# A two-layer hybrid diffusion step on one core: the second layer's modulation on VectorE, first loads as long rows, equal slots, and operands at chosen places of 256 bytes

## The chip, the cores and the metric

The kernel runs on one core of one Trainium2 chip. The time is device microseconds of one execution. The kernel before was run three times: 1936.15, 1937.8 and 1947.53 us, so its median is 1937.8 us. The profiled execution is a fourth run; times inside the trace (its span) are a little shorter than the device's own time for the same execution.

## The reference, cut to what matters

Two layers work on 384 tokens (128 context tokens, which are modulated by `c_ctx`, and 256 latent tokens, modulated by `c`) of 1024 channels. Each layer is

```python
shift1, scale1, gate1, shift2, scale2, gate2 = split(adaLN of c)
h = rms_norm(x) * (1 + scale1) + shift1
x = x + gate1 * mix(h)        # SSD, attention and mLSTM side by side, gated, one output projection
h = rms_norm(x) * (1 + scale2) + shift2
a, b = split(h @ w_ffn_in)    # 2 x 2816 wide
x = x + gate2 * ((silu(a) * b) @ w_ffn_out)
```

The six modulation vectors of a layer ("adaLN") are `silu(c) @ w_ada + b_ada`, with a matrix of 1024 x 6144 for each layer and two vectors (context and latent). All of it is float32.

## The kernel before, in words

A `Recorder` notes every operation first. `order()` then plays them through with its own list of costs and waiting times (`cost`, `LAT`, a model of TensorE's clock, one of the port that VectorE and GpSimd share, one of the DMA ring), takes on each engine the operation with the smallest key (its place in the program plus the `urgency` around it: FEED for loading and splitting weights, EVAC for emptying PSUM, DENSE for large products), and so writes down an order for each engine, which the chip then keeps. All instructions are issued from one line of `emit`, so the profile shows one line for all of them and is read by the names of tiles.

All weights stand in one array `in_ws` of pieces of 128 x 1024 float32 (512 KB), in the order in which `stream()` lists them. `piece()` loads a piece into one of four `raw` tiles; ACT rounds it to `wh` (the high part), and VectorE, or GpSimd for every n-th piece of the kinds in `POOL_SPLIT`, writes the rest to `wl`. A dense product of 128 output channels (`dense_t`) is 24 matmuls: eight chunks of 128 input channels, each `wh` by the activations' high part, `wh` by their low part and `wl` by their high part. The activations lie in large tiles by pairs (`HH`/`HL` for the mixers' input, `A`/`C` for the FFN's, `PH`/`PL` for a branch). There are three PSUM tiles `d` for dense products, four `m` and one `l` for small ones.

A layer goes through: early gates and the input projections with the three mixers between them (their steps taken by turns as the string `MIX` says: s is one group of two SSD heads, a attention, m mLSTM, q and i inputs), the three branch projections (`br`), the output projection (`outproj`), the FFN's first half (`fa` and `fb`, 22 times two dense products) and its second half (`fo`). After each dense product of the FFN's first half VectorE takes it out of PSUM times the norm (`sc<-d,nacc`); the product of the halves is again split into a high part (ACT) and a low part (VectorE), in the tiles `D`, `E`, `F`, `F2`, `B`, `HH`, `HL`.

The adaLN has three forms. Four units of layer 0 (`ada`: shift1 and scale1) are computed at the very start, because the first product needs them. The rest of layer 0 (`ada_step`, 16 steps) is spread over the branch and output projections, and all of layer 1 (`ada_step`, 24 steps) over the FFN of layer 0. A step takes two pieces and is four matmuls of the two modulation vectors (`silc`, as stationary operand, 32 columns) by 512 columns of weights in float32, side by side in four column groups of the array; after eight steps the result is transposed back and `b_ada` is added.

At the start, `setup` loads the small inputs and `x` (tile `PH`), the sums of squares of `x` run on ACT and VectorE (`ssq`, `norm_end`), the first four `ada` units come in through the four `raw` tiles, and `modulate` makes `HH`/`HL` chunk by chunk.

Of the kernel before, what the change touches and what calls it, by code (L numbers as in the profile page):

```python
# [21 lines left out]
LAYERS = 2  # L22
FFN = 2816
FT = FFN // P
EPS = 1e-6
# [5 lines left out]

EARLY_GATES = (0, 1, 2, 4, 5, 5, 6, 6, 6, 10, 11, 13, 13, 23, 32, 32, 32, 33, 33, 37, 37, 37, 37, 38)

# [30 lines left out]
def stream():  # L64

    s = [(("ada", 0, u), 4) for u in (0, 2, 1, 3)]
    steps = lambda l, *gs: [(("ada", l, g, k), 2) for g in gs for k in range(KT)]
    for l in range(LAYERS):
        early = iter(gates())
        s += [(("gate", l) + next(early), 1) for _ in range(FIRST_GATES if l else 0)]  # L70
        s += [(("dtmg", l), 1)]
        base = [(("in", l, OFF[n] + j * P), 1) for n in ("sx", "sb", "sc") for j in range(2 if n != "sx" else 8)]
        base += [(("inn", l, OFF["aq"] + j * 512), 4) for j in range(3)]
        base += [(("in", l, OFF[n] + j * P), 1) for n in ("mq", "mk") for j in range(8)]
        base += [(("inn", l, OFF["mv"] + j * 512), 4) for j in range(2)]
# [12 lines left out]
    return s  # L88
# [134 lines left out]
class Recorder:  # L223
# [122 lines left out]
    def cost(eng, meth, args, kw):  # L346
# [7 lines left out]
        if eng == "vector":  # L354
            if meth == "reciprocal":
                return 0.07 + n * 0.0062
            if meth == "tensor_reduce":
                n = _free(args[1])
            if meth == "tensor_scalar" and not args[1].buf.psum:
                n = n / 2  # L360
            return 0.07 + 0.06 * col * (n > 1) + n / 960.0
        if eng == "gpsimd":
            return 0.147 + n * 0.0021 if meth == "tensor_tensor" else 0.03 + n * 0.0009
        if eng == "sync":
            big, run = max(int(np.prod(v.shape)) for v in args[:2]), min(_run(v) for v in args[:2])
            rows = big / run
            return 0.36, rows * (0.025 + run * 4 * 0.0000415) / 16, 1.3 + min(rows, 256) * 0.0085

# [7 lines left out]
    def order(self):  # L376
# [24 lines left out]
        pe = self.Clock()  # L401
        port = ring = 0.0

# [124 lines left out]
FEED, EVAC, DENSE = -60000, -30000, 60000  # L528

ND, NM, NL = 3, 4, 1  # L530
NR = 4

AHEAD = 14


MIX = "sssiiiqqqsqqmamsasqamsasammmaamam"

POOL_SPLIT = {"inn": 4, "fa": 3, "fo": 3}


class Net:
    def __init__(self, ctx, tc, I, O):
# [7 lines left out]
        self.pools = {n: e(tc.tile_pool(name=n, bufs=1, **k)) for n, k in (  # L550
            ("cp", {}), ("wp", {}), ("sp", {}), ("rp", {}), ("pd", dict(space=PSUM)), ("pm", dict(space=PSUM)),
            ("pl", dict(space=PSUM)), ("dr", dict(space=DRAM)))}
# [14 lines left out]
    def slot(self, tag, shape, dt=F32):  # L567
        return self.buf("sp", tag, shape, 1, dt)

# [70 lines left out]
    def piece(self, key, split=True):  # L640
        while self.stream[self.spos][0] != key:
            ahead = self.stream[self.spos][0]
            (self.early_gate if ahead[0] == "gate" else self.ada_step)(*ahead)
        want, cnt = self.stream[self.spos]
        assert want == key, (want, key)
        out, kind = [], key[0]
        with self.urgency(FEED):
            for _ in range(cnt):
                raw = self.buf("wp", "raw", [P, 1024], NR)
                self.dma(raw, self.I["ws"][self.ppos])  # L650
                self.ppos += 1
# [81 lines left out]
    def ada(self, l, u):  # L733
        raws = self.piece(("ada", l, u), split=False)
        ps = self.dps()
# [9 lines left out]
        ps2 = self.dps()  # L745
        self.nc.tensor.transpose(ps2[:, 0:P], st, self.ident)
        src = ps2[:, 0:P].rearrange("p (j r) -> p j r", j=4)[:, :, 0:2]
        m = self.mod[l % 2][:, 4 * u:4 * u + 4, :]
# [5 lines left out]
    def ada_step(self, kind, l, g, k):  # L754
# [19 lines left out]
        for i, place in enumerate((2 * g, 2 * g + 1)):  # L774
# [3 lines left out]
            elif place in (GATE1, GATE2):  # L778
                self.ts(v, v, 0.5, ALU.mult)

    def setup(self):
        nc, I = self.nc, self.I
# [6 lines left out]
        self.ident = self.cst("ident")  # L789
        self.badas = []  # L790
        for l in range(LAYERS):
            b = self.const(f"bada{l}", [P, 48])
            self.dma(b, I["cols"][l, :, COLS["bada"][0]:COLS["bada"][0] + 48])
            self.badas.append(b)
        self.dma(self.x, I["xT"])
        self.ones = self.const("ones", [P, P])
        nc.gpsimd.memset(self.ones, 1.0)
# [4 lines left out]
        self.ts(ct, ct, 0.5, ALU.mult)  # L802
        self.stt(self.silc[:, :, 0:2], th, 1.0, ct, ALU.add, ALU.mult)
        self.mod = [self.const(f"mod{i}", [P, 48, 2]) for i in range(2)]
        self.cols = self.const("cols", [P, NCOL])
# [38 lines left out]
    def scaled(self, l, shift, scale, k):  # L844


        if k == 0:
            self.xs = [self.slot(t, [P, KT, NTOK + 2], F32R) for t in "AC"]
        hi, lo = self.xs
# [375 lines left out]
    def ml_inputs(self, l):  # L1225
        nc = self.nc
        self.mq = self.slot("C", [P, 8, NTOK])
        self.mk = self.slot("D", [P, 8, NTOK])
        self.mv = self.slot("E", [P, 3, 8, 129])
        for j in range(8):  # L1230
# [138 lines left out]
    def ffn(self, l):  # L1369
# [4 lines left out]
        for j in range(FT):  # L1374
# [10 lines left out]
            with self.urgency(EVAC):  # L1385
# [26 lines left out]
    def run(self):  # L1412
        self.setup()
        for u in (0, 2, 1, 3):
            self.ada(0, u)
        for j in range(8):
            self.ssq(self.x[:, j], j, self.tt)
        self.xd = self.I["xT"]
        for l in range(LAYERS):
# [7 lines left out]
            self.ts(self.mlnh, self.col("mln", 0, 8), 0.5, ALU.mult)  # L1427
            self.norm_end(EPS)
            self.gd = self.dram("gd", [P, 24, NTOK])
# [19 lines left out]
            self.outproj(l, m)  # L1449
            self.norm_end(EPS)  # L1450
            self.ffn(l)
# [48 lines left out]
def layout(a):  # L1500
# [17 lines left out]
    pos = 0  # L1518
    for key, n in st:
# [9 lines left out]
        elif kind == "ada":  # L1529
            v = w_ada[l, key[3]].reshape(P, 6, D)[:, [CHUNKS[2 * key[2]], CHUNKS[2 * key[2] + 1]]]  # L1530
        elif kind == "br":
            v = tiles(w_br[l, key[2]], key[3] * P)
# [8 lines left out]
        ws[pos:pos + n] = v.reshape(P, n, 1024).transpose(1, 0, 2)  # L1541
        pos += n
    out["ws"] = ws
    x = np.concatenate([A["x_prompt"].reshape(P, D), A["x_sample"].reshape(256, D)], axis=0)
# [63 lines left out]
```

## Time and profile before

| | |
|---|---|
| median of three runs | 1937.8 us |
| the profiled execution, device time | 1940.55 us |
| its span in the trace | 1938.4 us |
| TensorE busy | 1894.3 us (98%) |
| VectorE busy | 1290.6 us (67%) |
| ScalarE busy | 945.6 us (49%) |
| GpSimd busy | 367.1 us (19%) |
| read from HBM | 295.54 MB |

A TensorE that is shown busy for 98% is not one at its peak: matmuls overlap each other in the record, so the distance between two starts is what a matmul costs. A large product of 384 columns starts about every 0.17 us.

### The profile page before, as it was taken

Reading aid. Unit: us, or ns where it says so; the run is one execution under the profiler, and the core shown is the slowest. Engines: PE = TensorE matmul, PEld = TensorE weight load, DVE = VectorE, ACT = ScalarE, POOL = GpSimd, SP = SyncE. Lnnn points to the kernel's source line nnn. Section 1 sums busy time; section 2 is a strip of 40 time slices with the busy share of each in tenths; the row PEclk is TensorE's granted clock in tenths of the full one; section 3 lists DMA queues with packets and bytes.
Section 4 is the critical chain, followed back from the end, with each engine's and each line's share of the span. In section 5 each row is a group of like instructions: output and inputs, shape, how many; then the busy total and the mean of one; then the engine's idle time right before and its main releaser. Section 6 shows DMA issues by size and latency. Waiting matters only on the chain. (4 is left out here: it accounts for less than half of the span.)

```text
span 1938.4 us, 30576 instructions
## 1 busy us (share of the span) xinstructions
PE 1894.3 (98%) x11202; PEld 1728.1 (89%) x11202; DVE 1290.6 (67%) x2733; ACT 945.6 (49%) x1910; POOL 367.1 (19%) x355
## 2 busy tenths in 40 slices
PE   6999999999999999999999999999999999999997
PEld 4998898688888999999999978986889999999997
DVE  3856887986745666565348668978867567666622
ACT  3655565765422444444336546656655434444421
POOL 0115432210102210000211234322100022000121
PEclk9999999999999999999999999999999999999998
DMA  8466555554578666666654655555544555444441
GB/s 302 122 178 190 148 150 147 141 147 129 172 262 267 223 196 185 196 201 201 192 178 144 156 170 150 158 147 135 144 124 140 161 169 160 120 125 124 131 125 61
DMA packets 120342, 318.33 MB, mean 164 GB/s; under 512 B 13824, under 2 KB 57216, under 8 KB 119424
## 3 DMA queue, kind: packets, MB, share of 16 engines
q1 hardware_dynamic: 120192, 316.38, 54.8%
q8 instruction: 88, 1.44, 0.3%
q14 instruction: 62, 0.51, 0.1%
HBM read 295.54 MB, written 19.74 MB: 163 GB/s over the span
## 5 line engine op out<-in xcount | busy, mean ns | idle before, releaser
L509 ACT ACTIVATE wh<-raw 128x1024 fp32r<-128x1024 f32 x374 | 396.0, 1059 | 566.8 <-PE d L509 509.1
L509 DVE TENSOR_TENSOR wl<-raw,wh 128x1024 fp32r<-128x1024 f32 x335 | 437.3, 1306 | 247.3 <-ACT wh L509 240.4
L509 PE MATMUL d<-HH,wh 128*128 128x384 f32 x1448 | 493.0, 348 | 2.6 <-ACT sc L509 1.6
L509 PE MATMUL d<-HL,wh 128*128 128x384 f32 x1416 | 467.9, 336 | 1.4 <-DVE HL L509 1.4
L509 PE MATMUL d<-HH,wl 128*128 128x384 f32 x1384 | 465.6, 336 | 0.7 <-DVE wl L509 0.7
L509 PEld LDWEIGHTS d<-HH,wh 128*128 128x128 f32 x1448 | 272.6, 189 | 22.8 <-issue 14.8
L509 PEld LDWEIGHTS d<-HL,wh 128*128 128x128 f32 x1416 | 266.8, 189 | 3.2 <-DVE HL L509 1.7
L509 PEld LDWEIGHTS d<-HH,wl 128*128 128x128 f32 x1384 | 261.0, 189 | 1.1 <-DVE wl L509 1.1
L509 PE MATMUL d<-A,wh 128*128 128x386 f32 x744 | 254.8, 342 | 0.0
L509 PE MATMUL d<-C,wh 128*128 128x386 f32 x744 | 251.5, 338 | 0.0
L509 PE MATMUL d<-A,wl 128*128 128x386 f32 x744 | 250.1, 336 | 0.0
L509 POOL TENSOR_TENSOR wl<-raw,wh 128x1024 fp32r<-128x1024 f32 x39 | 93.9, 2409 | 449.6 <-ACT sh L509 361.3
L509 PEld LDWEIGHTS d<-A,wh 128*128 128x128 f32 x744 | 139.9, 188 | 13.0 <-issue 10.9
L509 PEld LDWEIGHTS d<-C,wh 128*128 128x128 f32 x744 | 140.6, 189 | 0.4
L509 PEld LDWEIGHTS d<-A,wl 128*128 128x128 f32 x744 | 139.9, 188 | 0.0
L509 POOL TENSOR_TENSOR sc<-sc,sc 128x126 f32<-128x126 f32 x112 | 66.7, 614 | 253.9 <-DVE sc L509 195.9
L509 DVE TENSOR_TENSOR sc<-d,nacc 128x384 f32<-128x384 f32 x93 | 51.8, 557 | 78.9 <-PE d L509 74.6
L509 DVE SCALAR_TENSOR_TENSOR PH<-PL,n,cst 128x128 f32<-128x128 f32 x288 | 95.9, 366 | 7.7 <-PE m L509 5.2
L509 PE MATMUL d<-wh,HH 128*128 128x512 f32 x240 | 98.2, 409 | 0.0
L509 PE MATMUL d<-wl,HH 128*128 128x512 f32 x240 | 93.9, 391 | 0.0
L509 PE MATMUL d<-wh,HL 128*128 128x512 f32 x240 | 93.8, 391 | 0.0
L509 DVE SCALAR_TENSOR_TENSOR sc<-d,cw,sc 128x127 f32<-128x127 f32 x224 | 79.2, 408 | 14.9 <-ACT sc L509 14.4
(237 smaller groups left out, 3080.1 us busy)
## 6 DMA issues: line engine op xcount, KB each, us to landing
raw<-in_ws SPq DMA_DIRECT2D x470, 512.0 KB, 3.9
PL<-rowr SPq DMA_DIRECT2D x48, 384.0 KB, 5.7
gd<-sc SPq DMA_DIRECT2D x48, 192.0 KB, 2.0
pb<-gd SPq DMA_DIRECT2D x48, 192.0 KB, 2.9
ex<-rowe SPq DMA_DIRECT2D x32, 128.0 KB, 4.1
ex<-rowe SPq DMA_DIRECT2D x16, 256.0 KB, 5.5
PH<-in_xT SPq DMA_DIRECT2D x2, 1536.0 KB, 7.2
yad<-pb SPq DMA_DIRECT2D x16, 192.0 KB, 3.0
```

Of the source, the lines that this page charges most:

```text
L509: tc.keep_in_program_order(getattr(engines[op.eng], meth)(*[real(a) for a in args], **{k: real(v) for k, v in kw.items()}))
```

## The change

Several parts are changed at once.

1. The adaLN of layer 1 leaves TensorE. Its 24 `ada_step` are replaced by 48 `ada_block` (`adv` in the stream). A block has one piece with 128 output channels on the partitions and the 1024 input channels along the row; VectorE multiplies it with the modulation vector, laid over all partitions (tile `PL`, filled from a copy in DRAM, `sild`), and sums along the row with `accum_out`, once for each of the two vectors. 32 blocks are spread over the FFN's first half, 16 over the second.
2. The first 16 pieces are loaded by six DMAs with rows of 8 or 12 KB into the tiles `A`, `C`, `E`, `F`, `D` and `PL` (`FIRST_LOADS`), not through the four `raw` tiles; their layout in DRAM is changed to match. `urgency` FIRST and SECOND set what is issued first, NORM puts the norms ahead of everything.
3. The large tiles get a pool of their own, with slots of one size for most of them. Two pads put `raw`, `wh` and `wl` at 0 modulo 256 bytes of a partition's row, and the large tiles at 64. In the program before, weights begin at 160; `HH`, `HL`, `A` and `D` at 160, `PH`, `PL`, `B` and `E` at 224, `F`, `F2` and `C` at 64.
4. Some numbers of the planner (a price for `accum_out`, DMA prices, the ring's start), the string `MIX`, one early gate, and `POOL_SPLIT`: GpSimd no longer splits pieces of `inn`, `fa` and `fb` but every second one of `fo`; in layer 0 it makes the low parts of the FFN's inner activations.

```diff
-EARLY_GATES = (0, 1, 2, 4, 5, 5, 6, 6, 6, 10, 11, 13, 13, 23, 32, 32, 32, 33, 33, 37, 37, 37, 37, 38)
+EARLY_GATES = (0, 1, 2, 4, 5, 5, 6, 6, 6, 10, 11, 13, 13, 23, 31, 32, 32, 32, 33, 33, 37, 37, 37, 38)
...
-        s += spread(ff, steps(l + 1, 0, 1)) + spread(fo, steps(l + 1, 2)) if l + 1 < LAYERS else ff + fo
+        if l + 1 < LAYERS:
+            blocks = [(("adv", l + 1, place, j), 1) for place in range(6) for j in range(8)]
+            at = len(blocks) * len(ff) // len(ff + fo)
+            s += spread(ff, blocks[:at]) + spread(fo, blocks[at:])
+        else:
+            s += ff + fo
...
+BIG = ("A", "B", "C", "D", "E", "F", "F2", "K", "HH", "HL", "PH", "PL")
+PADS = dict(p1=96, p2=64)
+FIRST_LOADS = ((0, 3, "A"), (3, 3, "C"), (6, 2, "E"), (8, 3, "F"), (11, 3, "D"), (14, 2, "PL"))
...
-MIX = "sssiiiqqqsqqmamsasqamsasammmaamam"
+MIX = "ssiiiqqqaqqmamsasqmssasasmmmaamam"
...
-POOL_SPLIT = {"inn": 4, "fa": 3, "fo": 3}
+POOL_SPLIT = {"fo": 2}
...
+    def ada_block(self, kind, l, place, j):
+
+        if self.spos == self.adv_at:
+            t = self.slot("PL", [P, 3, D])
+            self.dma(t[:, 0:2], self.sild.rearrange("r p k -> r (p k)").unsqueeze(0).to_broadcast([P, 2, D]))
+            self.silb = t
+        raw, = self.piece((kind, l, place, j), split=False)
+        with self.urgency(FEED):
+            for r in range(2):
+                self.nc.vector.scalar_tensor_tensor(self.silb[:, 2] if r == 0 else raw, raw, 1.0, self.silb[:, r],
+                                                    ALU.mult, ALU.mult, accum_out=self.mod_col(l, place, j, r))
...
-                self.tt(homes[j][:, 1], th, homes[j][:, 0].bitcast(F32), ALU.subtract)
+                (self.ptt if l == 0 else self.tt)(homes[j][:, 1], th, homes[j][:, 0].bitcast(F32), ALU.subtract)
```

What stands on the engines now. On SP's queue at the start of the program (`raw` are single pieces, `sil` and `cst` small inputs, `PH` is `x`), before:

```order
L509 DMA raw_80<-in_ws 128x1024
L509 DMA raw_84<-in_ws 128x1024
L509 DMA raw_86<-in_ws 128x1024
L509 DMA raw_88<-in_ws 128x1024
L509 DMA K_90<-in_ckT 128x128 x2
L509 DMA sil_2_93<-in_cT 128x16
L509 DMA cst_95<-in_cst 128x395
L509 DMA bada_4_97<-in_cols 128x48
L509 DMA bada_5_99<-in_cols 128x48
L509 DMA PH_101<-in_xT 128x3072
```

and after:

```order
L516 DMA sil_2_89<-in_cT 128x16
L516 DMA cst_97<-in_cst 128x395
L516 DMA PH_99<-in_xT 128x3072
L516 DMA A_101<-in_ws 128x3072
L516 DMA C_103<-in_ws 128x3072
L516 DMA E_105<-in_ws 128x2048
L516 DMA bada_4_107<-in_cols 128x48
L516 DMA bada_5_109<-in_cols 128x48
L516 DMA raw_111<-in_ws 128x1024
L516 DMA raw_113<-in_ws 128x1024
L516 DMA raw_115<-in_ws 128x1024
L516 DMA F_117<-in_ws 128x3072
```

The modulation vector and `x` have moved ahead of all weights; half of the first sixteen pieces, and then three pieces for the first dense products, follow as long rows and single tiles, with no tile that has to come free first; `D` and `PL` stand right behind.

On VectorE in the middle of the FFN's first half of layer 0 (`sc<-d,nacc` empties a dense product, `wl` splits a piece, `E` is the low part of an inner activation), before:

```order
L509 TENSOR_TENSOR sc_7882<-d_7829,nacc_7390 128x384
L509 TENSOR_TENSOR wl_7892<-raw_7759,wh_7880 128x1024
L509 SCALAR_TENSOR_TENSOR sc_7899<-sc_7899,sc_7882 128x384
L509 TENSOR_TENSOR sc_7922<-d_7876,nacc_7390 128x384
L509 SCALAR_TENSOR_TENSOR sc_7899<-sc_7922,sh_7927,sc_7899 128x128
L509 SCALAR_TENSOR_TENSOR sc_7899<-sc_7922,sh_7927,sc_7899 128x256
L509 TENSOR_TENSOR sc_7959<-d_7916,nacc_7390 128x384
L509 TENSOR_TENSOR wl_7968<-raw_7866,wh_7957 128x1024
L509 TENSOR_TENSOR E_7774<-sc_7899,E_7774 128x384
```

and after:

```order
L516 TENSOR_TENSOR wl_8096<-raw_8020,wh_8081 128x1024
L516 SCALAR_TENSOR_TENSOR PL_6956,mod_14_7104<-raw_8055,PL_6956 128x1024
L516 SCALAR_TENSOR_TENSOR sc_8102<-sc_8102,sc_8073 128x384
L516 SCALAR_TENSOR_TENSOR raw_8055,mod_14_7104<-raw_8055,PL_6956 128x1024
L516 SCALAR_TENSOR_TENSOR sc_8102<-sc_8085,sh_8090,sc_8102 128x128
L516 TENSOR_TENSOR wl_8138<-raw_8029,wh_8125 128x1024
L516 SCALAR_TENSOR_TENSOR sc_8102<-sc_8085,sh_8090,sc_8102 128x256
L516 SCALAR_TENSOR_TENSOR PL_6956,mod_14_7104<-raw_8108,PL_6956 128x1024
L516 TENSOR_TENSOR sc_8162<-d_8077,nacc_7422 128x384
L516 TENSOR_TENSOR sc_8170<-d_8121,nacc_7422 128x384
L516 SCALAR_TENSOR_TENSOR raw_8108,mod_14_7104<-raw_8108,PL_6956 128x1024
L516 TENSOR_TENSOR wl_8188<-raw_8064,wh_8168 128x1024
```

The two operations of each block (`PL,mod<-raw` and `raw,mod<-raw`) now stand between the splits and the emptying of PSUM; the operation on `E` is gone to GpSimd, and every piece is split here.

On GpSimd in layer 1, between the last convolutions of the SSD inputs (`sc<-sc,sc`) and the attention inputs (`E`); `ex` and `pb<-xn,we` prepare one group of two SSD heads, `PH` belongs to the decays, before:

```order
L509 TENSOR_TENSOR sc_11209<-sc_11209,sc_11216 128x254
L509 TENSOR_TENSOR PH_11239<-PH_11239 128x384 x3
L509 TENSOR_TENSOR ex_11363<-ex_11363,pb_11157 128x512
L509 TENSOR_TENSOR pb_11425<-xn_11401,we_10855 128x256
L509 TENSOR_TENSOR PH_11239<-PH_11239 128x384
L509 TENSOR_TENSOR wl_11492<-raw_11304,wh_11483 128x1024
L509 TENSOR_TENSOR E_11341<-E_11341,pT_5437 128x512
```

and after:

```order
L516 TENSOR_TENSOR ex_10809<-ex_10809,pb_11113 128x512
L516 TENSOR_TENSOR ex_10821<-ex_10821,pb_11113 128x512
L516 TENSOR_TENSOR sc_11166<-sc_11166,sc_11173 128x126
L516 TENSOR_TENSOR sc_11166<-sc_11166,sc_11173 128x254
L516 TENSOR_TENSOR PH_11196<-PH_11196 128x384 x4
L516 TENSOR_TENSOR E_11295<-E_11295,pT_5567 128x512
```

The third group of SSD heads, whose `ex` and `pb` stood here one behind the other, has left this place (the string `MIX` begins with two s now), and so has the split of a weight.

## Rows read from the trace of the kernel before

**Rows 1.** The page, part 1: busy time and instructions of each engine.

```profile
PE 1894.3 (98%) x11202; PEld 1728.1 (89%) x11202; DVE 1290.6 (67%) x2733; ACT 945.6 (49%) x1910; POOL 367.1 (19%) x355
```

**Rows 2.** Windows: layer 0 out, fa, fo; layer 1 fa, fo. Length, PE PEld DVE ACT POOL, clock.

```profile
662.10:698.00 35.90, 35.90 (x214) 33.72 (x212) 25.75 (x39) 17.09 (x31) 8.68 (x7) 1.00 0.70 221
698.60:905.30 206.70, 206.70 (x1200) 188.53 (x1200) 126.95 (x190) 91.81 (x183) 16.74 (x7) 1.00 0.61 192
905.60:1005.70 100.10, 100.10 (x588) 93.33 (x587) 38.06 (x50) 33.24 (x48) 23.12 (x13) 1.00 0.58 179
...
1644.40:1831.00 186.60, 186.60 (x1065) 186.19 (x1065) 125.76 (x184) 89.97 (x179) 19.14 (x8) 1.00 0.42 124
1831.30:1923.40 92.10, 92.10 (x534) 92.03 (x534) 23.96 (x32) 25.15 (x29) 20.39 (x12) 1.00 0.33 98
```

**Rows 3.** Timeline of PE around one adaLN step in layer 0's FFN: start, duration, instruction.

```profile
860.60 0.34 PE L509 MATMUL d<-A,wl 128*128 128x386 f32 x1
860.87 1.06 PE L509 MATMUL m<-raw,silc 128*32 128x512 f32 x8
861.86 0.44 PE L509 MATMUL d<-A,wh 128*128 128x386 f32 x1
862.14 0.34 PE L509 MATMUL d<-C,wh 128*128 128x386 f32 x1
```

**Rows 4.** Groups on VectorE in layer 0's fa stage: count, busy us, mean ns, idle before.

```profile
L509 DVE TENSOR_TENSOR wl<-raw,wh 128x1024 fp32r<-128x1024 f32 x37 | 45.4, 1226 | 12.8 <-ACT wh L509 12.7
L509 DVE TENSOR_TENSOR sc<-d,nacc 128x384 f32<-128x384 f32 x43 | 24.0, 557 | 46.5 <-PE d L509 44.4 <-ACT nacc L509 2.1
...
L509 DVE SCALAR_TENSOR_TENSOR sc<-sc,sh,sc 128x256 f32<-128x256 f32 x21 | 10.0, 477 | 0.0
...
L509 DVE SCALAR_TENSOR_TENSOR C<-PH,mod,A 128x128 fp32r<-128x128 f32 x1 | 0.3, 345 | 0.0
```

**Rows 5.** Timeline of VectorE in layer 1's fa stage.

```profile
1706.03 1.23 DVE L509 TENSOR_TENSOR wl<-raw,wh 128x1024 fp32r<-128x1024 f32 x1 [0.36 <-ACT wh L509]
1707.17 0.74 DVE L509 SCALAR_TENSOR_TENSOR sc<-sc,sh,sc 128x128 f32<-128x128 f32 x2
```

**Rows 6.** Timelines of VectorE and of GpSimd at 1553 us.

```profile
1553.43 1.82 DVE L509 TENSOR_TENSOR wl<-raw,wh 128x1024 fp32r<-128x1024 f32 x1 [0.36 <-ACT wh L509]
...
1553.14 1.02 POOL L509 TENSOR_TENSOR E<-E,pb 128x384 f32<-128x384 f32 x1 [0.60 <-DVE pb L509]
```

**Rows 7.** Groups on ACT: reading out a sum along the row.

```profile
L509 ACT ACTIVATION_READ_ACCUMULATOR pb<-m,st 128x1 f32 x64 | 12.8, 200 | 0.0
```

**Rows 8.** Windows at the start, and the first large matmul in PE's timeline.

```profile
4.00:20.00 16.00, 6.47 (x99) 4.83 (x99) 4.08 (x13) 3.88 (x11) 0.00 (x0) 1.00 1.03 385
20.00:36.00 16.00, 15.09 (x182) 9.48 (x174) 4.37 (x24) 1.80 (x6) 1.97 (x6) 1.00 0.89 306
...
40.00:45.00 5.00, 3.60 (x14) 3.28 (x13) 3.33 (x7) 1.36 (x2) 0.00 (x0) 0.73 0.96 267
...
38.00 0.44 PE L509 MATMUL d<-HH,wh 128*128 128x384 f32 x1 [1.03 <-ACT wh L509]
```

**Rows 9.** PE's timeline in layer 1 at a wait for GpSimd, and the window behind it.

```profile
1138.91 0.34 PE L509 MATMUL d<-HH,wl 128*128 128x384 f32 x1
1142.60 0.69 PE L509 MATMUL m<-pb,bn 128*64 128x128 f32 x4 [3.35 <-POOL pb L509]
...
1143.00:1148.00 5.00, 5.00 (x19) 4.78 (x16) 3.69 (x18) 1.12 (x2) 1.02 (x1) 0.50 0.63 147
```

**Rows 10.** Groups of large matmuls on PE over the whole span: count, busy us, mean ns.

```profile
L509 PE MATMUL d<-HL,wh 128*128 128x384 f32 x1416 | 467.9, 336 | 1.4 <-DVE HL L509 1.4
...
L509 PE MATMUL d<-A,wh 128*128 128x386 f32 x744 | 254.8, 342 | 0.0
...
L509 PE MATMUL d<-A,wl 128*128 128x386 f32 x744 | 250.1, 336 | 0.0
...
L509 PE MATMUL d<-PL,wh 128*128 128x384 f32 x256 | 86.0, 336 | 0.0
```

More of the change, by code (lines that the diff above doesn't have):

```diff
@@ L366, in cost @@
             rows = big / run
-            return 0.36, rows * (0.025 + run * 4 * 0.0000415) / 16, 1.3 + min(rows, 256) * 0.0085
+            return 0.36, rows * (0.036 + run * 4 * 0.0000337) / 16, 1.3 + min(rows, 256) * 0.0085
     LAT = dict(tensor=dict(tensor=0.0, scalar=0.21, vector=0.21, gpsimd=0.25, sync=0.25),
@@ L401, in order @@
         pe = self.Clock()
[L402 removed]
+        port, ring = 0.0, 2.2
         def offer(i, t):
@@ L649, in piece @@
                 raw = self.buf("wp", "raw", [P, 1024], NR)
-                self.dma(raw, self.I["ws"][self.ppos])
+                with self.urgency(FIRST if self.ppos < 16 + AHEAD_OF_SECOND else FEED):
+                    self.dma(raw, self.I["ws"][self.ppos])
                 self.ppos += 1
@@ L733, in ada @@
     def ada(self, l, u):
-        raws = self.piece(("ada", l, u), split=False)
+        key, cnt = self.stream[self.spos]
+        assert key == ("ada", l, u), key
+        self.spos += 1
+        if self.ppos % 8 == 0:
+            with self.urgency(SECOND if self.ppos else FIRST):
+                for pos, n, tag in FIRST_LOADS:
+                    if pos // 8 == self.ppos // 8:
+                        home = self.slot(tag, [P, n, 1024])
+                        self.dma(home.rearrange("p n c -> p (n c)"),
+                                 self.I["ws"][pos:pos + n].rearrange("n p c -> (n p c)").rearrange("(p m) -> p m", p=P))
+                        self.homes += [home[:, i] for i in range(n)]
+        raws = [self.homes.pop(0) for _ in range(cnt)]
+        self.ppos += cnt
         ps = self.dps()
@@ L746, in ada @@
         self.nc.tensor.transpose(ps2[:, 0:P], st, self.ident)
+        if u == 0:
+            with self.urgency(FIRST):
+                for i, b in enumerate(self.badas):
+                    self.dma(b, self.I["cols"][i, :, COLS["bada"][0]:COLS["bada"][0] + 48])
         src = ps2[:, 0:P].rearrange("p (j r) -> p j r", j=4)[:, :, 0:2]
@@ L789, in setup @@
         self.ident = self.cst("ident")
[L790 to L794, printed above, removed]
+        self.homes = []
+        self.badas = [self.const(f"bada{l}", [P, 48]) for l in range(LAYERS)]
         self.dma(self.x, I["xT"])
+        for n, size in PADS.items():
+            if size:
+                nc.gpsimd.memset(self.buf(n, n, [P, size // 4], 1), 0.0)
         self.ones = self.const("ones", [P, P])
@@ L803, in setup @@
         self.stt(self.silc[:, :, 0:2], th, 1.0, ct, ALU.add, ALU.mult)
+        rows = self.slot("sil2", [P, 2, KT])
+        self.act(rows, self.silc[:, :, 0:2].rearrange("p k r -> p r k"), AF.Copy)
+        self.sild = self.dram("sild", [2, P, KT])
+        with self.urgency(0):
+            self.dma(self.sild.rearrange("r p k -> p r k"), rows)
+        self.adv_at = [k[0] for k, _ in self.stream].index("adv")
         self.mod = [self.const(f"mod{i}", [P, 48, 2]) for i in range(2)]
@@ L1412, in run @@
     def run(self):
-        self.setup()
+        with self.urgency(FIRST):
+            self.setup()
         for u in (0, 2, 1, 3):
             self.ada(0, u)
-        for j in range(8):
-            self.ssq(self.x[:, j], j, self.tt)
+        with self.urgency(NORM):
+            for j in range(8):
+                self.ssq(self.x[:, j], j, self.tt)
         self.xd = self.I["xT"]
@@ L1427, in run @@
             self.ts(self.mlnh, self.col("mln", 0, 8), 0.5, ALU.mult)
-            self.norm_end(EPS)
+            with self.urgency(NORM):
+                self.norm_end(EPS)
             self.gd = self.dram("gd", [P, 24, NTOK])
@@ L1449, in run @@
             self.outproj(l, m)
-            self.norm_end(EPS)
+            with self.urgency(NORM):
+                self.norm_end(EPS)
             self.ffn(l)
@@ L1542, in layout @@
         pos += n
+    for at, n, _ in FIRST_LOADS:
+        ws[at:at + n] = ws[at:at + n].transpose(1, 0, 2).reshape(n, P, 1024)
     out["ws"] = ws
```

26 lines of the change are left out of this document (21 added, 5 removed).

## The prediction

> **What bounds the kernel now.** I read the page first, then windows by stage, then the timeline of TensorE (PE) where the adaLN steps stand. PE is busy for 98% of the span, VectorE for 67% [rows 1]. The windows show the same inside every stage that the change touches: in the FFN of layer 0 PE is busy for all of 206.7 and 100.1 us, at the full clock [rows 2]. So time goes away only where PE gets less to do, starts earlier, or loses a gap; work moved to VectorE is free as long as it fits beside PE. The two layers are each other's control: the FFN halves take 206.7 and 100.1 us in layer 0 and 186.6 and 92.1 us in layer 1, with the same products [rows 2]; what layer 0 has beyond them is mostly the adaLN of layer 1.
>
> **Layer 1's adaLN leaves PE.** The layers differ by 306.8 - 278.7 = 28.1 us for 24 steps, 1.17 us each. The timeline agrees: around one step two large matmuls start 1.54 us apart, from 860.60 to 862.14, where two ordinary distances are 0.35 us, so the step costs 1.19 us [rows 3]. PE thus loses 28.1 us of work.
>
> What VectorE gets: 96 operations on 128 x 1024, two float32 tiles in, one out, and a sum along the row. The trace has none with a sum. The nearest row without one is the split `wl`, same size: 1.23 us [rows 4], of which 0.08 overlap the next instruction (the next one starts 1.14 us after it [rows 5]). Reading out a sum costs 0.20 us on ACT [rows 7]; on VectorE I bound it by 0 and 0.20 and take 0.08, since its smallest instructions overlap too. So 1.22 us an operation, between 1.14 and 1.35.
>
> The fa stage of layer 0 on VectorE, each duration less 0.08: 44 splits at 1.14 (all of them now) are 50 us; 44 times PSUM out at 0.47 are 21; per half pair 0.47 + 0.26 + 0.39 (384, 128 and 256 columns), 22 times, 25; the norm and the rest 5: 101 us [rows 4, 5]. By the order 58 block operations stand between the first and the last `sc<-d,nacc`: 71 us. The 22 low parts that GpSimd takes over remove 10 us (already left out of the sum) but are not free: a split that meets a GpSimd operation of 1.02 us took 1.82 instead of 1.23 us [rows 6]; 22 times 0.6 are 13 us (0 if they meet PSUM reads, 22 if all of each is lost). Sum 185 us, between 167 and 201, against PE's 186.6. The out stage before it: VectorE is busy 25.8 us and gets 12 block operations, 14.6 us, so 40 of PE's 35.9. The fo stage: 24 us (layer 1's row) and 26 operations, 32 us, so 56 of 92. Over all three, 281 of 315 us: it fits, but out and fa together hold 225 us of work in 222.5 us. VectorE runs full there, each of its waits (for ACT's `wh`, for PSUM) is no longer covered, and behind a late `wl` or a late emptying of `d` PE itself is queued. I charge 6 us (0 to 20). **Net -22 us** (-28 to -8).
>
> One rule speaks against this part. In the trace an operation with a sum does not occur, and what rows show of two float32 inputs from SBUF is one speed: a scalar-tensor-tensor of 256 columns takes 477 ns and one of 128 takes 345, and a split of 1024 takes 1226 [rows 4], so 1.03 to 1.05 ns a column at any size. The Trainium skill (Vector Engine (DVE) Microarchitecture Reference, section 7, Points that are easy to get wrong) says that a scalar-tensor-tensor with two SBUF sources that are not bf16 runs at half throughput, because both read ports are taken and none is left for reading the accumulator back. The rows without a sum show no halving; no run here shows one with a sum. By that rule the sum below would end on the slower side; it is the second rival.
>
> **The start.** The first large matmul starts at 38.00 us [rows 8]. The queue moved 385 GB/s between 4 and 20 us but 306 GB/s between 20 and 36, when each piece had to wait for one of four `raw` tiles [rows 8]. In the changed order x, 16 pieces and three more are issued without such a wait: 0.2 + 1.5 + 19 x 0.5 MB, 11.7 million bytes, 30.5 us at 385 GB/s. From a start at about 2 us the last adaLN piece lands at 32.5; its two pieces' products on PE (16 records each, about 1.1 us) end at 34.6. By PE's order the large matmuls follow: 3.4 us earlier than before. By then four chunks of `HH`/`HL` and three split pieces are ready, 36 matmuls; before, PE did only 14 between 40 and 45 us, at 0.73 of the clock, waiting for chunks [rows 8], where 5 us hold 29 at full speed, so 2.6 us more are to be had. **-6 us** (-2 if the long rows load no faster, -8 if the clock does not fall).
>
> **The mixers.** At 1138.91 us PE waits 3.35 us for GpSimd's `pb`, and behind this idle time the granted clock is 0.50 (the 1.2 GHz level) through the next 5 us, which costs another 2.5 [rows 9]. In the new order the third group of SSD heads is gone from that place, and with it the wait; it comes later, between attention and mLSTM, where it may wait as well. I take 4 of the 5.9 us. Against this the new order changes 33 times more between float32 and split products (581 changes, where the old order without the 24 steps has 548). Behind such a change two large matmuls start 0.28 us apart (861.86 to 862.14) instead of 0.175 [rows 3]: +0.1 each, **+3.5 us**. The splits that GpSimd loses in the input projections and in layer 1's fa fall to VectorE, 8 x 1.14 = 9 us there, where it has 61 us free in 186.6 [rows 2]: nothing. For waits that I cannot see in the order I leave +-6. **-0.5 us** together.
>
> **Places in SBUF.** The question is whether a large matmul is faster with weights at 0 and activations at 64. Before, `HL` and its weights both begin at 160, and `PL` begins 64 behind its weights, the distance that all pairs now get; both show 336 ns [rows 10]. `A`, whose rows of 386 columns shift from chunk to chunk, shows 342 with `wh` and 336 with `wl` [rows 10]. If all of that is place, 744 x 6 ns = 4.5 us can be won; as much can be lost. I take **-1.5 us** (-4.5 to +4.5). DMA rows, ACT and VectorE with tiles at other places: no row shows a dependence, 0.
>
> **Sum.** -22 - 6 - 0.5 - 1.5 = -30 us. The profiled execution took 1940.55 us, 2.75 more than the median of the runs: 1910.5 us by its own time, 1907.8 against the median of 1937.8. **I predict 1908 us.**
>
> **Rivals.**
>
> First, VectorE does become the bound in out and fa: the read-out costs 0.20 and GpSimd's operations cost their full length. Then out and fa hold 42 + 201 = 243 us against 222.5, so 20 us instead of the 6 charged: 1922 us. For it: the sum above is full to the brim. Against it: in the order two reads of PSUM mostly stand side by side behind an inner activation, where GpSimd's operation costs VectorE nothing. 18%.
>
> Second, on the slower side: the sum halves the speed of the 96 operations. 1024 columns then take 1.07 us longer each (1.05 ns a column once more [rows 4]), 103 us in all; VectorE holds 281 + 103 = 384 us against PE's 315, and out to fo last 384 instead of 343 us before. That is +41 instead of -22: 1908 + 63 = 1971 us. It decides from 1.58 us an operation ((315 - 164) / 96) that PE waits at all, and from 1.95 ((343 + 8 - 164) / 96, the 8 us being the other terms) that the kernel is slower than before. For it: a sum has to be kept from column to column, and no row has one. Against it: all rows with two float32 inputs have the same price a column. The rule above would be a reason for it. 8%.
>
> Third, the parts beside the adaLN do not do what they say: the long rows load no faster (-2), the third group of heads waits elsewhere (0), changes cost 5, new waits 6, and the places cost 3: -22 - 2 + 5 + 6 + 3 = -10, so 1928 us. For it: most of PE's gaps are a few tenths each, and an order that mends one makes another. Against it: the first loads have nothing to wait for. 16%.
>
> The forecast, with PE still the bound and single terms off by some us (1892 to 1918), has 58%.
>
> **How the numbers follow.** A measurement of this kernel tells about 1% from no change, 19 us: faster means under 1918.4 us. The forecast gives 0.58 of that and the milder half of the first rival some 0.07: 0.65. The rest of the first rival and most of the third lie within 1%: 0.26. The second rival and a third one that goes worse: 0.09. The range leaves out the second rival and a little at both ends: 1892 (all terms at their good end, but for the adaLN's charge of 2) to 1932 us (first and third rival in part together).
>
> **What the new profile should show.** No `m<-raw,silc` behind some 700 us, and fa of layer 0 near 190 us, fo near 93. VectorE at over 90% in the fa window and its block operations at 1.2 to 1.35 us, with a read-out of their own beside them. The first `HH` matmul at 34 to 35 us. No wait of 3 us for `pb` in layer 1, and the clock at 1.00 there. The distance between large matmuls in fa at 0.174 to 0.176 us. I am wrong if the block operations take 1.6 us or more, if PE waits for `wl` or for an empty `d` in fa by more than 10 us, or if the distance of large matmuls moves by more than 1 ns: each ns is 8.7 us over 8736 of them.

## The result and the profile after

The changed kernel takes 1912.34 us (median of four runs, 1910.44 to 1913.74) against 1940.05 us before on the same chip: a ratio of 0.9852, 95% interval 0.9819 to 0.9885. 1908 was predicted, 1892 to 1932 as the range. Times and ratios here and below leave out the one execution that ran at a lowered clock throughout (it belongs to the fourth kernel of places). The profiled execution's span is 1912.0 us, 26.4 less than before.

The page, part 1, answers [rows 1]:

```profile
PE 1864.8 (98%) x10998; PEld 1726.6 (90%) x10998; DVE 1373.3 (72%) x2923; ACT 944.3 (49%) x1905; POOL 362.2 (19%) x362
```

PE has 29.5 us less to do, VectorE 82.7 more, and PE is still busy for 98%. The windows by stage (layer 0 out, fa, fo; layer 1 fa, fo; columns as in [rows 2]) are cut here at the starts of the large products:

```profile
660.50:694.10 33.60, 33.44 (x194) 33.15 (x193) 27.76 (x46) 15.56 (x27) 5.95 (x5) 1.00 0.71 241
694.10:889.20 195.10, 190.98 (x1071) 190.42 (x1072) 180.25 (x307) 89.21 (x181) 33.49 (x23) 0.99 0.64 205
889.20:981.40 92.20, 92.20 (x536) 92.20 (x535) 72.32 (x104) 34.37 (x50) 40.84 (x18) 1.00 0.63 206
...
1616.50:1805.00 188.50, 188.50 (x1065) 188.13 (x1065) 119.32 (x191) 91.23 (x179) 2.40 (x1) 1.00 0.39 122
1805.00:1896.90 91.90, 91.90 (x533) 91.78 (x533) 19.09 (x28) 25.16 (x29) 30.04 (x16) 1.00 0.31 98
```

The second half of layer 0 is now as long as that of layer 1; the first half is 6.6 us longer than layer 1's, and layer 1's own first half, cut at the same products in both kernels, has grown from 186.9 to 188.5 us. VectorE is busy for 92% of layer 0's fa.

The whole difference by stages, cut at the starts of the first large products of each (start to first product; hh are the mixers with their projections, br the branches):

| stage | before | after | difference |
|---|---|---|---|
| start | 38.0 | 35.0 | -3.0 |
| hh, layer 0 | 503.8 | 503.8 | 0.0 |
| br, layer 0 | 120.4 | 121.7 | +1.3 |
| out + fa + fo, layer 0 | 343.7 | 320.9 | -22.8 |
| hh, layer 1 | 504.9 | 501.3 | -3.6 |
| br, out, layer 1 | 133.8 | 133.8 | 0.0 |
| fa, layer 1 | 186.9 | 188.5 | +1.6 |
| fo, layer 1, and the tail | 107.0 | 107.0 | 0.0 |

The sum is -26.5 us. Each column is one execution. In the experiments below that keep the changed kernel's order of large products there and its places, hh of layer 1 takes 499.8 to 503.1 us and br of layer 0 120.7 to 123.8, and two kernels with the same order and the same distance of operands differ by 4.8 us in br (123.7 and 118.9). So differences of 3 us in these rows can come from the execution alone. The start's gain is larger than its row: at the 120th large product the new kernel leads by 7.4 us, at the end of hh by 2.9.

VectorE's timeline between two halves shows what a block operation costs (start, duration, instruction):

```profile
701.05 1.21 DVE L516 SCALAR_TENSOR_TENSOR PL<-raw,PL 128x1024 f32<-128x1024 f32 x1
702.20 0.07 DVE L516 DVE_READ_ACCUMULATOR PL<-raw,PL 128x1 f32 x1
702.20 0.15 DVE L516 TENSOR_SCALAR rs<-rs 128x3 int32<-128x3 int32 x1
...
706.77 2.36 DVE L516 TENSOR_TENSOR wl<-raw,wh 128x1024 fp32r<-128x1024 f32 x2 [0.45 <-ACT wh L516]
709.05 1.22 DVE L516 SCALAR_TENSOR_TENSOR PL<-raw,PL 128x1024 f32<-128x1024 f32 x1
710.19 0.08 DVE L516 DVE_READ_ACCUMULATOR PL<-raw,PL 128x1 f32 x1
710.19 1.22 DVE L516 TENSOR_TENSOR wl<-raw,wh 128x1024 fp32r<-128x1024 f32 x1
711.33 1.22 DVE L516 SCALAR_TENSOR_TENSOR raw<-raw,PL 128x1024 f32<-128x1024 f32 x1
712.47 0.08 DVE L516 DVE_READ_ACCUMULATOR raw<-raw,PL 128x1 f32 x1
712.47 1.48 DVE L516 TENSOR_TENSOR sc<-d,nacc 128x384 f32<-128x384 f32 x3
```

The operation lasts 1.21 to 1.22 us here; the sum's read-out of 0.08 us lies beside the start of the next instruction, which comes 1.14 us after the operation began (1.15 once), as behind a split [rows 5]. Of all 96, the 58 that meet no GpSimd operation last 1.22 us on average and at most; the 38 that meet one last 1.62 us on average, up to 2.95. The rule of the Trainium skill that the prediction set against this part (Vector Engine (DVE) Microarchitecture Reference, section 7, Points that are easy to get wrong) is not what the trace shows: with two float32 sources in SBUF and a sum, 1024 columns run at the speed of a split, not at half of it.

The same rows show the one place in fa where the full VectorE reaches PE: two splits, two block operations and another split stand ahead of the first `sc<-d,nacc` at 712.47, and PE, with all three `d` full, waits for it. PE's timeline, and the window behind the wait:

```profile
708.71 0.34 PE L516 MATMUL d<-A,wl 128*128 128x386 f32 x1
713.17 0.41 PE L516 MATMUL d<-A,wh 128*128 128x386 f32 x1 [4.12 <-DVE sc L516]
```

```profile
714.00:719.00 5.00, 5.00 (x21) 5.00 (x20) 4.42 (x8) 2.22 (x5) 1.38 (x1) 0.66 0.41 155
```

Behind the wait the clock is granted at 0.66 for 5 us. The wait (4.1 us) and that clock (a third of 5 us) make 5.8 of the 6.6 us by which fa of layer 0 exceeds that of layer 1. The windows at the start answer [rows 8]:

```profile
4.00:20.00 16.00, 7.94 (x93) 6.62 (x97) 6.29 (x23) 4.23 (x11) 0.00 (x0) 1.00 1.00 414
20.00:32.00 12.00, 6.38 (x136) 4.24 (x132) 9.14 (x23) 7.03 (x14) 0.00 (x0) 0.99 1.01 423
...
40.00:45.00 5.00, 5.00 (x31) 5.00 (x30) 3.09 (x10) 3.06 (x7) 2.41 (x6) 1.00 0.21 77
```

The queue moves 414 to 423 GB/s between 4 and 32 us, and between 40 and 45 us PE runs 31 products at full clock, where it ran 14 at 0.73. The groups of large products answer [rows 10]; two of those with 512 columns (input projections with the weights as moving operand) are added, which the prediction did not look at:

```profile
L516 PE MATMUL d<-HL,wh 128*128 128x384 f32 x1416 | 469.3, 337 | 0.0
L516 PE MATMUL d<-A,wh 128*128 128x386 f32 x744 | 255.4, 343 | 4.3 <-DVE sc L516 4.1 <-ACT A L516 0.2
L516 PE MATMUL d<-A,wl 128*128 128x386 f32 x744 | 252.8, 340 | 0.0
L516 PE MATMUL d<-wh,HL 128*128 128x512 f32 x240 | 95.0, 396 | 0.0
L516 PE MATMUL d<-wl,HH 128*128 128x512 f32 x240 | 95.0, 396 | 0.0
L516 PE MATMUL d<-PL,wh 128*128 128x384 f32 x256 | 86.1, 336 | 0.0
```

The same two before:

```profile
L509 PE MATMUL d<-wl,HH 128*128 128x512 f32 x240 | 93.9, 391 | 0.0
L509 PE MATMUL d<-wh,HL 128*128 128x512 f32 x240 | 93.8, 391 | 0.0
```

### The profile page after: what moved, and what is told of

It reads as the page before. It is cut to its first block, busy times and chain, and to the rows that moved or that the text cites. A ratio compares the mean times of both kernels' runs of the same rounds, so it can differ in the third digit from the quotient of the medians.

```text
span 1912.0 us, 30336 instructions
## 1 busy us (share of the span) xinstructions
PE 1864.8 (98%) x10998; PEld 1726.6 (90%) x10998; DVE 1373.3 (72%) x2923; ACT 944.3 (49%) x1905; POOL 362.2 (19%) x362
## 5 line engine op out<-in xcount | busy, mean ns | idle before, releaser
L516 DVE TENSOR_TENSOR wl<-raw,wh 128x1024 fp32r<-128x1024 f32 x352 | 454.9, 1293 | 226.3 <-ACT wh L516 223.6
L516 POOL TENSOR_TENSOR sc<-sc,sc 128x126 f32<-128x126 f32 x112 | 61.7, 569 | 272.4 <-DVE sc L516 159.7
L516 DVE SCALAR_TENSOR_TENSOR PH<-PL,n,cst 128x128 f32<-128x128 f32 x288 | 100.2, 381 | 14.6 <-PE l L516 5.3
L516 POOL TENSOR_TENSOR wl<-raw,wh 128x1024 fp32r<-128x1024 f32 x22 | 56.6, 2571 | 269.2 <-ACT sh L516 193.1
L516 PE MATMUL d<-PH,wh 128*128 128x384 f32 x256 | 87.2, 340 | 0.0
L516 PE MATMUL d<-PH,wl 128*128 128x384 f32 x256 | 86.1, 336 | 0.0
```

The costliest lines, as they stand in the source:

```text
L516: tc.keep_in_program_order(getattr(engines[op.eng], meth)(*[real(a) for a in args], **{k: real(v) for k, v in kw.items()}))
```

## The experiments

All are edits of the changed kernel. The theory: the adaLN on VectorE and the start carry the gain, VectorE's room decides the first, and the new places in SBUF cost time. The rivals stand with each expectation. Times are medians; the ratio is to the kernel before on the same chip.

**Layer 1's adaLN back on TensorE.**

```diff
-        if l + 1 < LAYERS:
...
-        else:
-            s += ff + fo
+        s += spread(ff, steps(l + 1, 0, 1)) + spread(fo, steps(l + 1, 2)) if l + 1 < LAYERS else ff + fo
```

> Layer 1's adaLN is back on TensorE in 24 steps; start, order of the mixers, places and the splits are as in the changed kernel. Theory: the 23 us that the stages of layer 0 from the output projection on became shorter are this part alone; they come back, less nothing: 1935 us, with 28 us of work on TensorE more and the wait of 4.1 us gone. Rival: the shorter stages came partly from the splits that GpSimd gave up or from the norm's place in the order; then the whole takes 1922 us or less.

1934.96 us, ratio 0.9979 (0.9968 to 0.999). Windows of layer 0's out, fa and fo:

```profile
660.70:697.60 36.90, 36.90 (x216) 34.35 (x216) 25.73 (x39) 17.16 (x31) 8.81 (x7) 1.00 0.68 222
697.60:906.20 208.60, 208.60 (x1201) 190.15 (x1200) 109.91 (x175) 92.47 (x183) 23.59 (x22) 1.00 0.61 191
906.20:1006.20 100.00, 100.00 (x588) 93.25 (x588) 36.21 (x46) 33.27 (x48) 31.95 (x17) 1.00 0.59 180
```

24.6 us come back in just these stages, which now take 345.5 us against 343.7 before: the splits and the norm, which stayed as changed, gave nothing there that can be seen. The theory holds; this part alone is most of the gain, and all the other parts together are worth 0.2%.

**Three times the work for the first vector.**

```diff
-            for r in range(2):
+            for r in (0, 0, 0, 1):
```

> Each block operation for the first of the two vectors is done three times instead of once (the same result three times), so VectorE has 96 operations of 1.14 us more, 109 us; the price per needed operation is 2.28 us, above the 1.58 from which the prediction says that TensorE waits. Theory (VectorE's room decides): VectorE was busy 279 us of the 319.5 us of the output projection and FFN of layer 0, so 388 us are needed there and the kernel is some 70 us longer, about 1980 us. Rival (the blocks lie beside TensorE's work whatever they cost, or the time goes by another limit such as the loads): under 20 us more.

2006.29 us, ratio 1.0332 (1.0317 to 1.0348). Out, fa and fo of layer 0:

```profile
661.20:695.10 33.90, 33.90 (x200) 33.90 (x199) 30.01 (x47) 17.70 (x32) 9.35 (x7) 1.00 0.62 218
695.10:954.30 259.20, 212.05 (x1066) 205.72 (x1067) 251.20 (x430) 85.91 (x174) 27.40 (x20) 0.89 0.52 155
954.30:1073.90 119.60, 103.00 (x536) 97.72 (x535) 112.46 (x163) 34.46 (x51) 42.92 (x19) 0.93 0.52 159
```

The columns have changed places: VectorE is busy for 251 of 259 us and PE for 212, at 0.89 of the clock. VectorE's work was right (394 us, 388 expected); the time is 92 us longer in these stages, not 70: the three stages last 412.7 us, so VectorE, now the bound, still stands idle for 19 of them, and PE's clock falls in PE's gaps. So the prediction's second rival was right in the direction of its consequence, left out this idle time, and lacked its cause.

**No block ahead of the FFN's norm.**

```diff
-            s += spread(ff, blocks[:at]) + spread(fo, blocks[at:])
+            s += ff[:6] + spread(ff[6:], blocks[:at]) + spread(fo, blocks[at:])
```

> The first three pairs of pieces of the FFN of layer 0 get no block of layer 1's adaLN, so that no block stands ahead of or inside the norm of the FFN on VectorE; the 32 blocks of the first half follow behind that. Theory: the one wait of TensorE for the first emptied dense product (4.1 us at 713 us) and the lower clock behind it (about 2.4 us) came from the blocks that VectorE did ahead of it; both go, the first half of the FFN of layer 0 gets 5 us shorter, 1907 us. Rival: VectorE is so full in the first half (180 of 195 us busy, and now some 6 block operations more) that the wait only comes later, between the pairs: no gain, 1912 us, or a loss.

1911.76 us, ratio 0.9853 (0.9833 to 0.9872): no gain. The wait at 713 us is gone and the clock stays at 1.00 there, as the theory says. But the window of fa then holds 182 us of VectorE's work in 193, and PE waits behind its product of 811.45 instead (2.5 us), for VectorE, on which four block operations and a split stand between two emptyings of `d` at 806.62 and 813.64; fo grows by 1.8 us. The cause of the wait was right, the gain was given back: the rival's point.

**GpSimd's share of the inner low parts back on VectorE.**

```diff
-                (self.ptt if l == 0 else self.tt)(homes[j][:, 1], th, homes[j][:, 0].bitcast(F32), ALU.subtract)
+                self.tt(homes[j][:, 1], th, homes[j][:, 0].bitcast(F32), ALU.subtract)
```

> The low parts of the FFN's inner activations of layer 0 go from GpSimd back to VectorE: 22 operations of 0.47 us more there (10 us), and no GpSimd operation that stretches VectorE's in the first half but those of single pieces. Theory: what GpSimd takes over is worth as much as it costs by stretching (about 13 us worked out in the prediction), so VectorE stays near 180 of 195 us and the time within 2 us of 1912. Rival: VectorE, busy for 92% there, has no room for 10 us more: 3 to 8 us longer.

1915.74 us, ratio 0.9872 (0.9853 to 0.9891), 3.4 us more by the medians, with overlapping intervals. In fa VectorE gets 4.3 us more to do (184.6 for 180.3, where 22 x 0.47 = 10 are moved, so by this sum 6 come back as less stretching), and the stage grows by 1.4 us; what the profiles differ by beyond it lies in stages that the edit doesn't touch (br of layer 0 +1.2, hh of layer 1 +1.8). By that sum GpSimd's operations cost VectorE more than half of what they take over; the two expectations are not told apart.

**Places in SBUF.** Four pairs of pads, nothing else changed. Weights and large tiles then begin, modulo 256, at 160 and 160, 0 and 0, 0 and 128, 160 and 224, where the changed kernel has 0 and 64:

```diff
-PADS = dict(p1=96, p2=64)
+PADS = dict(p1=0, p2=0)
...
+PADS = dict(p1=96, p2=0)
...
+PADS = dict(p1=96, p2=128)
...
+PADS = dict(p1=0, p2=64)
```

> Only the pads are gone: weights and large tiles all begin at 160 modulo 256, every order of instructions is as in the changed kernel. Theory: the places cost time in the changed kernel, since from before to after the three products of an FFN chunk (386 columns) went from 527 to 532 ns together and the products of 512 columns with the weights as moving operand from 228 to 233 ns. Then both go back to their values of before, the first half of the FFN of layer 1 is 186.6 instead of 188.1 us and the whole takes about 1905 us (3.4 and 3.6 us less than 1912). Rival: the places do nothing, and the spacing grew for another reason (order of the products, traffic of other engines): both stay at 532 and 233 ns, 1912 us.

> Weights at 0 and large tiles at 0: distance 0 as in e1, but another place. If what counts is the distance between the operands, this behaves as e1 (527 and 228 ns if e1 shows these). If what counts is the place of the weights alone, it behaves as the changed kernel (532 and 233 ns). If places do nothing, all four kernels of this call are within 1 ns at both products and within 2 us.

> Weights at 0, large tiles at 128: distance 128. By the distance, a third value at both products, different from distance 0 and 64; by the place of the weights alone, 532 and 233 ns as in the changed kernel; by nothing, no change (1912 us).

> Weights at 160, large tiles at 224: the distance of 64 that the changed kernel has, both moved by 160. By the distance, the changed kernel's values (532 and 233 ns, 1912 us); by the place of the weights, those of e1; by nothing, no change.

| weights, tiles | us | ratio (interval) | 386 columns, three products | 512 | 384 (`HL`) |
|---|---|---|---|---|---|
| before | | | 527.5 | 228.3 | 173.7 |
| 0, 64 (changed) | 1912.34 | 0.9852 (0.9819 to 0.9885) | 532.2 | 233.3 | 173.7 |
| 160, 160 | 1907.88 | 0.9837 (0.982 to 0.9854) | 529.7 | 228.1 | 173.9 |
| 0, 0 | 1907.69 | 0.9843 (0.9827 to 0.9859) | 529.6 | 228.1 | 173.9 |
| 0, 128 | 1919.18 | 0.9897 (0.9881 to 0.9913) | 530.4 | 232.4 | 176.0 |
| 160, 224 | 1909.01 | 0.9846 (0.9829 to 0.9862) | | | |

The last three columns are mean distances in ns between the starts of neighbouring large products, of those under 270 ns. The page's groups say the same; of the second kernel and of the third:

```profile
L516 PE MATMUL d<-wh,HL 128*128 128x512 f32 x240 | 93.7, 390 | 0.0
```

```profile
L516 PE MATMUL d<-HL,wh 128*128 128x384 f32 x1416 | 471.3, 338 | 0.0
L516 PE MATMUL d<-wh,HL 128*128 128x512 f32 x240 | 94.6, 394 | 0.0
```

The two kernels with distance 0 agree in every column within 0.1 ns though their places differ, and weights at 0 give 228 ns with the tiles at 0 and 233 with the tiles at 64: the place of the weights alone does not decide. At distance 64 the products of 512 columns take 5 ns more and those of 384 the same; at 128 both take more. Layer 1's fa goes from 188.5 to 187.6 us, not to the 186.9 of before: of the 386-column products' loss of 744 x 4.7 ns = 3.5 us some 1.6 have another cause, which the pads do not reach. By the medians distance 0 is worth 4.5 us against the changed kernel; by the ratios, each against the kernel before on its own chip, 1.7 to 2.9 us. These intervals overlap, so the rows carry the reading; only 128 against 0 is told apart by the whole time. The fourth kernel's profiled execution had a clock of 0.655 (span 2611.4 us), so its rows can't be set beside the others, and its time (1909.01 us, the median of three) overlaps with all but that of 128. So it is not shown that the distance decides and not the place of the large tiles alone: they were quick at 0 and 160, slow at 64 and 128.

**The old order of the mixers.**

```diff
-MIX = "ssiiiqqqaqqmamsasqmssasasmmmaamam"
+MIX = "sssiiiqqqsqqmamsasqamsasammmaamam"
```

(and `EARLY_GATES` as before.)

> The order of the mixers' steps and the gates among them are as before (the third group of SSD heads is back ahead of the attention inputs), all else as in the changed kernel. Theory: the new order costs layer 0 about 5.5 us in small waits and wins layer 1 about 3.8 us (the wait of 3.35 us for the low part from GpSimd and the half clock behind it), so the old one gives 1910 us, with that wait back in layer 1. Rival: the loss in layer 0 comes from the earlier start or from the splits that went from GpSimd to VectorE, not from the order: then layer 0 stays as it is, layer 1 loses 4 us, 1916 us.

1912.45 us, ratio 0.9853 (0.9836 to 0.9869). PE's timeline in layer 1 and the window behind it:

```profile
1111.76 0.34 PE L516 MATMUL d<-HH,wl 128*128 128x384 f32 x1
1115.29 0.44 PE L516 MATMUL m<-pb,bn 128*64 128x128 f32 x4 [3.19 <-POOL pb L516]
```

```profile
1115.00:1120.00 5.00, 4.71 (x26) 4.23 (x27) 3.02 (x14) 2.56 (x4) 1.25 (x2) 1.00 0.52 139
```

The wait of [rows 9] is back, and one like it in layer 0 at 167 us; but this time, in layer 1, the clock stays at 1.00, hh there takes 498.4 us, 2.9 less than with the new order, and layer 0's 503.6. Both expectations fall: layer 0 does not win 5.5 us, layer 1 does not lose 4. The order is worth nothing that can be measured.

**The first pieces through the `raw` tiles again.**

```diff
-FIRST_LOADS = ((0, 3, "A"), (3, 3, "C"), (6, 2, "E"), (8, 3, "F"), (11, 3, "D"), (14, 2, "PL"))
+FIRST_LOADS = ()
...
+        raws = self.piece(("ada", l, u), split=False)
```

> The first 16 pieces come through the four single tiles again, one DMA each, with the order that sets small inputs and x ahead of them; all else as in the changed kernel. Theory: the long first loads into tiles of their own are the start's gain, 7 us by the 120th large product; it comes back whole: first large product at 38 us, 1919 us. Rival: the mixers' stage waits on other engines and eats a lead anyway (of the lead of 7.4 us some 1.9 are left where it ends in the changed kernel): 1914 us or less, with a shorter mixers' stage.

1922.26 us, ratio 0.9907 (0.9891 to 0.9923). The windows at the start:

```profile
4.00:20.00 16.00, 7.71 (x78) 5.52 (x79) 6.62 (x27) 3.95 (x11) 0.00 (x0) 1.00 0.91 327
20.00:32.00 12.00, 7.99 (x119) 4.63 (x123) 5.99 (x19) 4.29 (x10) 2.07 (x6) 0.77 0.86 306
...
40.00:45.00 5.00, 3.22 (x9) 2.72 (x10) 3.63 (x7) 3.46 (x5) 0.00 (x0) 0.50 0.85 310
```

The queue is back at 306 to 327 GB/s and the clock at 0.50; the first large product starts at 41.5 us, hh ends 8.2 us later than in the changed kernel, the whole 9.9 us later. The start's gain is not eaten by the mixers; the rival falls. (It starts later than the kernel before, so the new order of loads without the long ones is a loss.)

**Two versions put together.** Both with the places 0, 0 and no block ahead of the norm; the second also does four blocks in the output projection.

```diff
+            s += ff[:6] + spread(ff[6:], blocks[:28]) + spread(fo, blocks[28:])
...
+            s += out[:4] + spread(out[4:], blocks[:4]) + ff[:6] + spread(ff[6:], blocks[4:30]) + spread(fo, blocks[30:])
```

> Both operands at 0 modulo 256 (as e2), no block ahead of the FFN's norm (as e5), and 28 instead of 32 of the 48 blocks in the first half, so that VectorE is less full there (9 us of work go to the second half, where it has 20 us free). Theory: the two gains add up, 4.5 us by the places and 4 by the wait that goes without a new one: 1904 us. Rival: the second half, or the first, gets a new wait, and only the places count: 1908 us.

> As e11, but four blocks are done in the output projection of layer 0, where VectorE has 9 us free of 34, 26 in the first half of the FFN behind the norm and 18 in the second half. Theory: VectorE has room in all three, no wait over 1 us is left in them: 1902 us. Rival: a block operation of 1.14 us ahead of an emptying of PSUM or of the norm's sums delays TensorE wherever it stands: 1906 us or more, with a wait of over 2 us somewhere between 655 and 980 us.

The first takes 1905.18 us, ratio 0.9823 (0.9807 to 0.9839), the fastest here. Its fa and fo of layer 0:

```profile
694.30:881.90 187.60, 187.60 (x1066) 187.22 (x1065) 175.46 (x295) 87.36 (x175) 30.11 (x21) 1.00 0.67 206
881.90:976.40 94.50, 92.97 (x536) 92.13 (x536) 85.64 (x122) 33.78 (x51) 40.09 (x18) 1.00 0.71 224
```

The first half takes 187.6 us, to the tenth what layer 1's takes, with 28 blocks spread over it; the places are not the cause, for with them alone (0, 0) it took 195.3. The second half pays 2.3 us (1.2 of them one wait for GpSimd). The second version takes 1914.21 us, ratio 0.9869 (0.9851 to 0.9886). Its output projection:

```profile
658.20:700.80 42.60, 35.55 (x200) 35.26 (x199) 33.98 (x55) 17.15 (x31) 8.01 (x7) 0.92 0.63 216
```

VectorE waits 2.0 us for x there, `PL` lands at 669.1 us, just ahead of the first block (10.3 us after its issue; 10.4 in the changed kernel), and then eight block operations and four splits stand on VectorE from 669 to 685 us ahead of the emptying of `d`, and PE stands for 7.0 us, as the rival said. VectorE is not seen to wait for `PL`; what put the order out of step is not shown. Its second half needs 92.2 us with 18 blocks, where the version with 20 took 94.5 us, the experiment without blocks ahead of the norm 94.0 with 16 and the changed kernel 92.2 with 16: the number alone does not decide.

## Why the prediction was right, point by point

**The adaLN: -22 predicted, about -24.5 measured** (-22.8 in its stages, with +1.7 of places inside them; 24.6 in the experiment). Operation and bound were right: 1.14 us from start to start instead of 1.22, where no GpSimd operation meets it, and VectorE at 92%. The charge of 6 us came true by its size (6.6), though not spread over many late splits: 5.8 of it are the one wait behind the norm and the clock after it. What made the term larger is its first number. The step took 28.1 us from the two FFN halves for all 24 steps; the trace of before has two of them in the output projection, which in layer 0 takes 36.5 us and in layer 1 33.9 (windows of layer 0's out, fa and fo, for the `silc` products alone, eight records a step):

```profile
662.10:698.60 36.50, 2.17 (x16) 0.35 (x16) 0.00 (x0) 0.00 (x0) 1.00 0.71 223
698.60:905.60 207.00, 17.05 (x128) 2.52 (x128) 0.00 (x0) 0.00 (x0) 1.00 0.61 192
905.60:1005.80 100.20, 6.39 (x48) 0.94 (x48) 0.00 (x0) 0.00 (x0) 1.00 0.58 180
```

With these 2.6 us PE loses 30.7 us, and 30.7 - 6.6 = 24.1 fits what was measured. The 28.1 us belong to 22 steps, 1.28 us each, so the 1.17 that seemed to agree with the timeline's 1.19 came from a wrong divisor. That VectorE decides is shown by the tripled work, and that the charge in fa can be had back by the first combined version.

**The start: -6 predicted, -7.4 measured** at the 120th product. That it hangs on the long loads is shown by taking them away, which costs 9.9 us, more than the gain.

**The mixers: -0.5 predicted, about -1.4 by the stages, less than single executions differ by; the mechanism of the step was wrong.** hh of layer 0 loses 4.5 us after the 120th product, 1.8 of them places; br loses 1.3; hh of layer 1 wins 3.6 against 1.8 of places: 2.7 + 1.3 - 5.4. The step said that the gap of [rows 9] goes with the order and 4 us with it. With the old order the gap is there again and layer 1 is just as fast; what shortened hh of layer 1 (PE idle in it for 9.0 us before, 5.4 after, 5.8 with the old order) is not the order; the splits that GpSimd gave up or the planner's prices may be it. Neither was tried apart, so it stays open. That the term came out near is luck.

**The places: -1.5 predicted, about +7 by the rows, some 5.6 of it by the pads; this term had the wrong sign.** Its step asked of `A`, `HL` and `PL` in [rows 10] whether distance 64 helps, and left out the products of 512 columns, whose moving operand is the weights. From before to after those lose 720 x 5.0 ns = 3.6 us, and those of 386 columns 3.5 us, together beyond the bound of 4.5. Distance 0 takes back 720 x 5.2 ns = 3.7 and 744 x 2.6 ns = 1.9 us of it; the rest has a cause that stays open, and in the whole time 1.7 to 4.5 us are seen. The products of 384 columns, on which the step did look, kept their distance. The prediction's own sign of being wrong, a distance that moves by more than 1 ns, came true for these two forms (5.0 ns at 512 columns, 1.6 on average over the three products of 386), while over all 8736 the two losses make 0.8 ns.

The four add up to -26.3 us, where -30 was predicted: three terms came out 4.8 us better, one 8.5 worse. So the total lies 4.4 us from the measured median partly because errors of both signs met, which is luck. The first rival (VectorE the bound, 20 us) fell: the read-out hides, and fa lost 6.6 us. The second fell at its cause; its column price was misread too, for [rows 4] give 0.98 to 1.03 ns a column and not 1.03 to 1.05. Of the third only the places came true.

## What to carry to other kernels

Work of the bound engine that fitted beside it on another engine was worth nearly its full time here, with that engine busy for 93% of the stage, once its pieces no longer stood ahead of the few instructions that the bound engine waits for. Look at the first emptying of PSUM behind a serial chain, such as a norm, and keep fillers behind it; moving them alone gave nothing here, and moving them with fewer of them in the full stage did. Eight fillers ahead of one emptying stood before a wait of 7.0 us, in a stage where VectorE was busy for only 34.0 of 42.6 us. Before tiles are shifted in SBUF, each form of product should be looked at by the distance of its starts, the rarer forms too. And before a cost is divided by a count, the trace should be asked in which stages the counted steps lie.

## What the runs showed of the hardware that was not expected

Reading out a sum along the row costs VectorE nothing that can be seen: its 0.08 us lie beside the next instruction. On ACT it has a row of 0.20 us [rows 7], and the next instruction starts 0.09 us after that row begins (the median of 144), so even there the row's length is not its cost.

A scalar-tensor-tensor of 1024 columns on VectorE lasts 1.22 us alone and 2.04 us beside one GpSimd operation of 384 columns (1.64 us) that overlaps it for 0.96 us.

The places of a product's two operands in SBUF, modulo 256 bytes, change the distance of starts: at a distance of 0 between them 228 ns and at 64 233 for 512 columns; 174 at 0 and 64 but 176 at 128 for 384. Whether the distance or the place of the large tiles does it is open.

What the clock does behind one and the same wait of 3.2 to 4.1 us differs from case to case: granted at 0.50 in [rows 9], 0.66 behind the wait in fa, 1.00 at the place of [rows 9] in the kernel with the old order. A price for a wait that includes the clock is right only on average.
